# Hybrid decoder trunk on one core: the odd layer in two token ranges, with less MLP filler per round

## The chip, the cores and the metric

The kernel runs on one core of a Trainium2 chip. The metric is the device time of one execution in microseconds (us); lower is better. The time before is 2784.98 us, the median of three executions from 2773.43 to 2786.07 us. The traced execution took 2783.84 us.

The engines are named as in the profile: PE (TensorE, the matmuls) with PEld (its weight loads), DVE (VectorE), ACT (ScalarE), POOL (GpSimd), and SP, whose queue issues the DMAs. `Lnnn` is a line of the kernel.

## The reference

Two layers over 1024 tokens of width 1024, each a mixer and then a squared-ReLU MLP (width 4096), each behind an RMSNorm. The even layer's mixer (sparse attention and pooling) is not touched. What matters is the odd layer, a gated DeltaNet, cut to its core:

```python
p = h @ w_in                                    # q, k, v, z: 8 heads of 128 each; b, a: one per head
qkv = silu(causal_depthwise_conv(qkv, conv_w))  # 4 taps along the tokens
q = l2norm(q) * 128 ** -0.5;  k = l2norm(k)
beta = sigmoid(b);  g = cumsum(-exp(a_log) * softplus(a + dt_bias))   # per head
tmat = inverse(I + strict_lower(beta * (k k^T) * decay))              # per chunk of tokens
value = tmat @ (v * beta);  k_cumdecay = tmat @ (k * beta * exp(g))
# chunk after chunk, with a 128x128 state per head:
v_new = val - kcd @ state;  o = qd @ state + at @ v_new
state = state * gl + kd^T @ v_new
y = (rmsnorm(o, o_norm) * silu(z)) @ w_out
h = h + y
h = h + square(relu(rmsnorm(h, mlp_norm) @ w1)) @ w2
```

The kernel takes chunks of 128 tokens, so each range of 512 tokens has four.

## The kernel before, in words

Tokens lie in two ranges of 512, `s = 0` and `s = 1`; the residual `h[s]` is eight 128x512 tiles. All wide products are made of three matmuls at 128x512 (`mm3`, lines L245, L246, L247): high part by high part, high by low, low by high. Each 128x512 tile of weights is loaded by a DMA into `raw`, copied to its high part by ACT (L165), and its low part is subtracted by POOL (L169). The projections of the odd layer and its output use weight tiles named `w`, the MLP uses `wm`.

`odd_heads` runs 16 head jobs, eight for each range. A head job (`odd_head`) is a generator of 17 steps, a chain that goes back and forth between PE, DVE and ACT: transposes (L977, L989, L995), the decay matrix (L1004 is one matmul per head and serves below as the head's mark), the products of keys and queries (L1018, L1020), the inversion by levels (L1044 and L1050 four times, L1070 and L1074 twice), four chunks through the state (L1088 to L1097) and the output transposes (L1116). Up to three head jobs are in flight, started at least eight rounds apart. In a round every active head makes a step, an output product (`output`, rows `ps_d<-y,w` and `ps_d<-yh,w`) may make two, a projection for a later head (`project`, rows `ps_g<-x,w`) may make one, and a share of MLP work, the filler, is written in between so that PE has something to do while a head's chain is on another engine.

The filler is `mlp_half`, the MLP of one layer on one range: per piece either 24 matmuls of the first product (rows `ps_g<-xb,wm` or `ps_g<-x,wm`, priced `T_COLS` = 5.6) or 6 of the second (rows `ps_d<-y,wm`, priced `T_ROWS` = 1.4). There are two: "below" is the even layer's MLP on range 1, which must end before the odd layer can read `h[1]`; "above" is the odd layer's MLP on range 0, which needs all of `h[0]`'s odd-layer output. `FILL = (5.6, 4.7)` is what a round gets while "below" and while "above" is in use.

The 16 head jobs form one list: the projection of range 1's head 0 may start while range 0's heads 6 and 7 are under way. Before it, all that is left of "below" is written out, then the norm of `h[1]` (`norm_stages`: squares, their sums by matmuls at L288, a reciprocal root in small DVE steps at L264 to L269, its spread over the partitions by transposes at L276, then eight scaled and split tiles). "above" starts when range 0's four output products are done; its own norm goes first. What is left of "above" after the last head goes beside the last norm of `h[1]`, and then the odd layer's MLP on range 1 runs alone.

The text in which the program is written is not the final order: a scheduler moves instructions, so that single filler matmuls stand between the small ones of a head. The order is told below.

Of the kernel before, what the change touches and what calls it, by code (L numbers as in the profile page):

```python
# [25 lines left out]
NH = 8  # L26
# [5 lines left out]
TOPK = 256  # L32
LEVELS = (2, 4, 8, 16, 32, 64)
STAGGER = 8
FILL = (5.6, 4.7)
EARLY = 7
BANKS = {"even": {"g": 2, "o": 1, "s": 1, "t": 4}, "odd": {"g": 2, "o": 1, "d": 2, "t": 3}}

# [11 lines left out]
R_MIX = 0  # L50
R_MLP = 16
# [73 lines left out]
class Trunk:  # L125
# [123 lines left out]
    def project(self, key, x, cols=P, tag="g", st="a"):  # L249

        ps = self.bank(tag)
        for n, w in enumerate(self.columns(key, st, cols)):
            for j in range(KT // 2):
                k = n * KT // 2 + j
                self.mm3(ps[:cols], w[0][:, j], w[1][:, j], x[k][:, 0:512], x[k][:, 512:1024], k == 0, k == KT - 1)
        self.tick(self.pace)
        return ps
# [865 lines left out]
    def odd_heads(self, fills):  # L1123


        seq = [(s, h) for s in range(2) for h in range(NH)]
        x, G, qkvz, ys = [[], []], [None, None], {}, {}
        outs, written = deque(), [0, 0]

        def project(i):  # L1130
            s, h = seq[i]
            if h == 0 and s == 1:
                yield from self.norm_stages(self.h[s], R_MIX + 8, x[s])
                yield
            t = []
            for n in range(4):
                while self.live == self.Q.n:
                    yield
                t.append(self.odd_project(s, h, n, x[s]))
                yield  # L1140
                if h == 0 and n == 1:
                    G[s] = self.odd_gates(x[s], self.grow)
                    yield
            qkvz[i] = t

        def output(s, h):
            for _ in range(5):
                yield
            a = [ys.pop((s, h - 1 + n)) for n in range(2)]
            yield from self.accumulate(("oo", s, h // 2), "o", a, s)  # L1150
            written[s] += 1

        def head(i):
            s, h = seq[i]
            yield from self.odd_head(s, h, *qkvz.pop(i), G[s], ys)
            if h % 2:
                outs.append(output(s, h))

        def step(gen):
            return next(gen, self) is not self  # L1160

        self.live = 0
        norm = self.norm_stages(self.h[0], R_MIX + 8, x[0])
        ahead, nxt, fill, due, above = None, 2, fills[0](), 0.0, False
        for n in (4, 2, 2):
            next(norm, None)
            for _ in range(n):
                next(fill)
        for _ in chain(project(0), project(1)):
            next(fill)  # L1170
        active, started, done, age = [], 0, 0, 0
        while done < len(seq) or outs:
            if started in qkvz and (not active or (len(active) < 3 and age >= STAGGER)):
                active.append(head(started))
                started, age = started + 1, 0
            age += 1
            for g in list(active):
                if not step(g):
                    active.remove(g)
                    done += 1  # L1180
            for _ in range(2):
                if outs and not step(outs[0]):
                    outs.popleft()
            if not above and fill is None and written[0] == NH // 2:
                fill, due, above = fills[1](), 0.0, True
            if fill:
                due += FILL[above]
                while fill and due > 0:
                    t = next(fill, None)
                    if t is None:  # L1190
                        fill = None
                    else:
                        due -= t
            if ahead is None and nxt < len(seq) and nxt < done + 3:
                if seq[nxt] == (1, 0) and fill:
                    for _ in fill:
                        pass
                    fill = None
                ahead, nxt = project(nxt), nxt + 1
            if ahead and not step(ahead):  # L1200
                ahead = None
        self.room("m", self.WM)
        while any(t[3] is not self.WM for t in self.ready["m"]):
            next(fill)
        return fill
# [188 lines left out]
    def run(self):  # L1394
        a, b = self.odd_units()
        m = [self.mlp_units(l) for l in range(2)]
        early, rest = self.mlp_units(0, 0, EARLY, 4), self.mlp_units(0, 2 * EARLY)
        self.plan(a=self.even_units() + a, o=b, m=early + rest + m[0] + m[1] + m[1])
        self.after_early = len(rest) + 3 * len(m[0])
        self.h = [[None] * KT, [None] * KT]  # L1400
        with ExitStack() as st:
            self.banks("even", st)
            self.even()
        self.banks("odd", self.stack)
        XB = Ring(self.pool("second"), "xb", 8, 1024)
        x = []
        norm = self.norm_stages(self.h[1], R_MLP, x, XB)

        def rest():
            fill = self.mlp_half(0, 0, self.x0, [self.Y], 2 * EARLY)  # L1410
            for n in (0, 2, 3):
                for _ in range(n):
                    yield next(fill)
                next(norm, None)
            yield from fill

        self.alone(rest(), "below", 3 * len(m[0]))
        below = lambda: self.mlp_half(0, 1, x, [self.Y])

        def above():  # L1420
            xa = []
            for _ in self.norm_stages(self.h[0], R_MLP + 8, xa, XB):
                yield FILL[1]
            yield from self.mlp_half(1, 0, xa, [self.Y])

        fill, x = self.odd([below, above]), []
        for _ in self.norm_stages(self.h[1], R_MLP + 8, x):
            for _ in range(4):
                next(fill, None)
        for _ in fill:  # L1430
            pass
        self.finish(0)
        self.alone(self.mlp_half(1, 1, x, [self.Y]), "above", 0)
        self.finish(1)
# [59 lines left out]
```

## Time and profile before

| | |
|---|---|
| median of three executions | 2784.98 us |
| the profiled execution | 2783.84 us |
| its span, first to last instruction | 2782.1 us |
| mean granted PE clock over the span | 0.978 of full |
| PE busy | 2653.8 us, 95% of the span |
| DVE, ACT, POOL busy | 60%, 43%, 44% |
| odd layer's head jobs, first to last head mark (L1004) | 1016.6 to 2203.0 us |
| MLP of range 1 alone at the end | from about 2425 us |

The span is 1.7 us below the execution's own time. PE's busy time joins overlapping records: matmuls follow each other faster than one record lasts, so a "busy" PE is not one at its peak. The granted clock is a mean over the stretch; 1.00 means it was never lowered there.

### The profile page before, as it was taken

To read this page: it belongs to the slowest core of one execution; us is meant where nothing else is said; L and a number is where in the kernel's file an instruction comes from. 1 tells how busy PE (TensorE), PEld (TensorE's weight loads), DVE (VectorE), ACT (ScalarE), POOL (GpSimd) and SP (SyncE) were. 2 spreads that over 40 slices of the span, in tenths; PEclk is the share of its full clock that TensorE was granted. 3 is DMA by queue.
4 is the path that set the end of the run, shared out by engine and by line. 5 is a ranking of instruction groups with operands and counts; after the bars stand their busy time and mean duration, and the time that the engine had idled before them with its cause. 6 is when DMAs were issued, how large, how long until landed. Compare 5 with 4: busy or idle time off the path is not lost. (4 is left out here: it accounts for less than half of the span.)

```text
span 2782.1 us, 44603 instructions
## 1 busy us (share of the span) xinstructions
PE 2653.8 (95%) x16640; PEld 2094.9 (75%) x16640; DVE 1660.1 (60%) x3587; ACT 1185.8 (43%) x2480; POOL 1227.5 (44%) x1062
## 2 busy tenths in 40 slices
PE   8789989999999999999999999999999999899998
PEld 6566768787777787777777767777777777688886
DVE  5788998734435655655565777655556645633334
ACT  4557767334444543433333344433334333433332
POOL 4653354542245444434454444434444434544442
PEclk9999989999999999999999999999999999999999
DMA  5221223331123222222222212122222222333332
GB/s 192 76 75 35 68 81 98 91 91 54 42 76 96 80 84 73 80 77 78 68 88 73 62 47 64 59 65 77 75 71 73 69 69 87 118 98 95 96 98 76
DMA packets 121068, 220.91 MB, mean 79 GB/s; under 512 B 14098, under 2 KB 15250, under 8 KB 120850
## 3 DMA queue, kind: packets, MB, share of 16 engines
q1 hardware_dynamic: 120850, 218.05, 25.4%
q8 instruction: 131, 2.15, 0.3%
q14 instruction: 87, 0.71, 0.1%
HBM read 209.61 MB, written 4.19 MB: 77 GB/s over the span
## 5 line engine op out<-in xcount | busy, mean ns | idle before, releaser
L169 POOL TENSOR_TENSOR wm<-raw,wm 128x512 fp32r<-128x512 f32 x425 | 562.0, 1323 | 853.9 <-ACT wm L165 840.3
L165 ACT ACTIVATE wm<-raw 128x512 fp32r<-128x512 f32 x425 | 267.3, 629 | 606.2 <-PE ps_g L246 270.7
L169 POOL TENSOR_TENSOR w<-raw,w 128x512 fp32r<-128x512 f32 x222 | 296.7, 1337 | 351.3 <-ACT w L165 330.8
L841 DVE TENSOR_TENSOR h<-ps_d,h 128x512 f32<-128x512 f32 x392 | 267.1, 685 | 134.4 <-PE ps_d L247 132.4
L245 PE MATMUL ps_g<-x,w 128*128 128x512 f32 x644 | 259.5, 403 | 12.1 <-ACT w L165 9.1
L827 DVE SCALAR_TENSOR_TENSOR ps_g<-ps_g,temps 128x512 f32<-128x512 f32 x128 | 89.1, 696 | 291.0 <-ACT temps L825 291.0
L246 PE MATMUL ps_g<-x,w 128*128 128x512 f32 x644 | 257.1, 399 | 4.3 <-DVE x L380 4.1
L247 PE MATMUL ps_g<-x,w 128*128 128x512 f32 x644 | 256.6, 398 | 1.0 <-POOL w L169 1.0
L245 PE MATMUL ps_d<-y,wm 128*128 128x512 f32 x596 | 243.7, 409 | 10.3 <-DVE h L841 8.7
L165 ACT ACTIVATE w<-raw 128x512 fp32r<-128x512 f32 x222 | 139.0, 627 | 258.3 <-PE ps_g L246 180.9
L247 PE MATMUL ps_d<-y,wm 128*128 128x512 f32 x596 | 236.5, 397 | 0.3 <-POOL wm L169 0.2
L246 PE MATMUL ps_d<-y,wm 128*128 128x512 f32 x596 | 236.0, 396 | 0.0
L245 PE MATMUL ps_g<-xb,wm 128*128 128x512 f32 x512 | 207.7, 406 | 5.6 <-ACT qkvz L947 5.0
L247 PE MATMUL ps_g<-xb,wm 128*128 128x512 f32 x512 | 206.4, 403 | 5.5 <-POOL wm L169 5.4
L246 PE MATMUL ps_g<-xb,wm 128*128 128x512 f32 x512 | 205.7, 402 | 0.0
L949 DVE SCALAR_TENSOR_TENSOR qkvz<-temps,conv,qkvz 128x512 f32<-128x512 f32 x144 | 130.8, 909 | 97.9 <-ACT qkvz L947 96.8
L245 PEld LDWEIGHTS ps_g<-x,w 128*128 128x128 f32 x644 | 123.2, 191 | 40.6 <-ACT w L165 9.9
L245 PE MATMUL ps_g<-x,wm 128*128 128x512 f32 x352 | 141.5, 402 | 7.7 <-ACT wm L165 2.9
L246 PEld LDWEIGHTS ps_g<-x,w 128*128 128x128 f32 x644 | 123.0, 191 | 33.3 <-DVE x L380 6.6
L245 PEld LDWEIGHTS ps_d<-y,wm 128*128 128x128 f32 x596 | 112.0, 188 | 44.9 <-DVE h L841 16.9
L246 PE MATMUL ps_g<-x,wm 128*128 128x512 f32 x352 | 140.9, 400 | 4.4 <-DVE x L169 4.4
L247 PE MATMUL ps_g<-x,wm 128*128 128x512 f32 x352 | 141.1, 401 | 3.2 <-POOL wm L169 3.2
(445 smaller groups left out, 6089.5 us busy)
## 6 DMA issues: line engine op xcount, KB each, us to landing
raw<-in_w_dram SPq DMA_DIRECT2D x456, 256.0 KB, 2.7
raw<-in_woi_dram SPq DMA_DIRECT2D x128, 256.0 KB, 2.6
raw<-in_w2q_dram SPq DMA_DIRECT2D x56, 256.0 KB, 2.6
raw<-in_wei_dram SPq DMA_DIRECT2D x52, 256.0 KB, 2.7
raw<-in_weo_dram SPq DMA_DIRECT2D x32, 256.0 KB, 2.7
raw<-in_woo_dram SPq DMA_DIRECT2D x32, 256.0 KB, 2.7
h<-in_xt_dram SPq DMA_DIRECT2D x16, 256.0 KB, 3.0
at<-at SPq DMA_DIRECT2D x64, 64.0 KB, 2.0
```

The lines of the kernel that those rows point to most:

```text
L165: self.nc.scalar.activation(out, in_, AF.Copy)
L169: eng.tensor_tensor(lo, full, hi.bitcast(F32), op=OP.subtract)
L245: mm(ps, wh, xh, start=start, stop=False)
L246: mm(ps, wh, xl, start=False, stop=False)
L247: mm(ps, wl, xh, start=False, stop=stop)
L827: nc.vector.scalar_tensor_tensor(ps, ps, 0.0, r, op0=OP.max, op1=OP.mult)
L841: nc.vector.tensor_tensor(h, ps, h, op=OP.add)
L949: nc.vector.scalar_tensor_tensor(acc, pin[:, j:j + 512], cw(j), acc, op0=OP.mult, op1=OP.add)
```

## The change

`odd_heads` becomes a loop over the two ranges. In each range: the norm of `h[s]` with 4, 2 and 2 filler pieces in its three stages, the projections of head 0 with a filler piece at each step, and then rounds until all eight heads and their outputs are done. There are no heads of both ranges in flight together any more. A round's filler is 3.5 when no projection is under way at that point and 2.8 when one is. After range 0, the norm for "above" stands with four pieces of "below" in each of its stages, all the rest of "below" is written out, and "above" becomes the filler from then on, so that it lies beside the norm of `h[1]` and the first projections of range 1. The normed input of range 1 goes into the ring `XB` that "below" read from, and "above" reads from `self.X`; before it was the other way round. The last norm also writes into `XB`.

No arithmetic is added or left out: there are as many matmuls as before.

```diff
-FILL = (5.6, 4.7)
+FILL = (3.5, 2.8)
...
-        seq = [(s, h) for s in range(2) for h in range(NH)]
-        x, G, qkvz, ys = [[], []], [None, None], {}, {}
-        outs, written = deque(), [0, 0]
-        def project(i):
-            s, h = seq[i]
-            if h == 0 and s == 1:
-                yield from self.norm_stages(self.h[s], R_MIX + 8, x[s])
-                yield
...
+        def filled(us):
+            self.due += us
+            while self.due > 0:
+                self.due -= next(fill, 1e9)
...
-        for _ in chain(project(0), project(1)):
-            next(fill)
-        active, started, done, age = [], 0, 0, 0
-        while done < len(seq) or outs:
...
-            if not above and fill is None and written[0] == NH // 2:
-                fill, due, above = fills[1](), 0.0, True
-            if fill:
-                due += FILL[above]
...
-            if ahead is None and nxt < len(seq) and nxt < done + 3:
-                if seq[nxt] == (1, 0) and fill:
-                    for _ in fill:
-                        pass
-                    fill = None
-                ahead, nxt = project(nxt), nxt + 1
+        for s in range(2):
+            self.due, G = 0.0, {}
+            norm = self.norm_stages(self.h[s], R_MIX + 8, xs[s], (self.X, self.XB)[s])
+            for n in (4, 2, 2):
+                next(norm, None)
+                for _ in range(n):
+                    next(fill)
+            for _ in project(s, 0, G):
+                next(fill)
+            active, started, done, age, ahead, nxt = [], 0, 0, 0, None, 1
+            while done < NH or outs:
...
+                filled(FILL[ahead is not None])
+                if ahead is None and nxt < NH and nxt < done + 3:
+                    ahead, nxt = project(s, nxt, G), nxt + 1
...
+            if s == 0:
+                xa = []
+                norm = self.norm_stages(self.h[0], R_MLP + 8, xa)
+                for _ in range(3):
+                    next(norm, None)
+                    for _ in range(4):
+                        next(fill, None)
+                for _ in fill:
+                    pass
+                fill = fills[1](xa)
...
-        def above():
-            xa = []
-            for _ in self.norm_stages(self.h[0], R_MLP + 8, xa, XB):
-                yield FILL[1]
-            yield from self.mlp_half(1, 0, xa, [self.Y])
+        above = lambda xa: self.mlp_half(1, 0, xa, [self.Y])
...
-        for _ in self.norm_stages(self.h[1], R_MLP + 8, x):
+        for _ in self.norm_stages(self.h[1], R_MLP + 8, x, XB):
```

How the order moves, at two places. The first is PE at the norm of `h[1]` ahead of range 1's heads, between the sums of squares (L288) and the spread of the root (L276). Before (`y,w` and `yh,w` are the output product of range 0, the others head work):

```order
L288 MATMUL ps_t<-ca,temps 128x2 x4
L246 MATMUL ps_d<-yh,w 128x512
L247 MATMUL ps_d<-yh,w 128x512
L245 MATMUL ps_d<-y,w 128x512
L1070 MATMUL ps_t<-xx_7986,lm 64x64 x4
L246 MATMUL ps_d<-y,w 128x512
L247 MATMUL ps_d<-y,w 128x512
L1074 MATMUL ps_t<-dy,xt 64x64 x4
L1004 MATMUL ps_t<-grow,sel 128x512
L276 MATMUL ps_t<-ca,rs_y 128x128 x4
```

Five wide matmuls and some head work stood between the two. In the changed program, at the same norm (`y,wm` and `x,wm` are the filler "above"):

```order
L288 MATMUL ps_t<-ca,temps 128x2 x4
L245 MATMUL ps_d<-y,wm 128x512
L246 MATMUL ps_d<-y,wm 128x512
L247 MATMUL ps_d<-y,wm 128x512
...
L276 MATMUL ps_t<-ca,rs_y 128x128 x4
L245 MATMUL ps_g<-x,wm 128x512
L246 MATMUL ps_g<-x,wm 128x512
L247 MATMUL ps_g<-x,wm 128x512
```

Eighteen filler matmuls stand there now, and 24 more between L276 and the first projection that reads the normed tiles.

The second place is PE within a range 0 head's window (from the mark L1004 of the range's head 2 to that of head 3), between the end of one level of the inversion (L1050) and the start of the next (L1044), which waits for two DVE steps. Before:

```order
L1050 MATMUL ps_t<-dy,xtc 32x16 x16
L246 MATMUL ps_d<-y,wm 128x512
L247 MATMUL ps_d<-y,wm 128x512
L245 MATMUL ps_d<-y,wm 128x512
...
L1088 MATMUL ps_t<-state,qkvz 128x128
L1093 MATMUL ps_o<-state,qkvz 128x128
L1044 MATMUL ps_t<-xxc,lm 32x16 x16
```

Twenty filler matmuls stood between the two levels. In the changed program:

```order
L1050 MATMUL ps_t<-dy,xtc 32x16
L247 MATMUL ps_d<-y,wm 128x512
L245 MATMUL ps_d<-y,wm 128x512
L246 MATMUL ps_d<-y,wm 128x512
L1088 MATMUL ps_t<-state,qkvz 128x128
L1093 MATMUL ps_o<-state,qkvz 128x128
L1044 MATMUL ps_t<-xxc,lm 32x16 x12
```

Three are left between them; in the same window the filler falls from 190 wide matmuls to 102.

More of the change, by code (lines that the diff above doesn't have):

```diff
@@ L1123, in odd_heads, with step @@
     def odd_heads(self, fills):
-        seq = [(s, h) for s in range(2) for h in range(NH)]
-        x, G, qkvz, ys = [[], []], [None, None], {}, {}
-        outs, written = deque(), [0, 0]
-        def project(i):
-            s, h = seq[i]
-            if h == 0 and s == 1:
-                yield from self.norm_stages(self.h[s], R_MIX + 8, x[s])
-                yield
[L1135 to L1144, printed above, removed]
+        xs, fill = [[], []], fills[0]()
+        qkvz, ys, outs, written = {}, {}, deque(), [0, 0]
+        def step(gen):
+            return next(gen, self) is not self
         def output(s, h):
@@ L1151, in output, with head @@
             written[s] += 1
-        def head(i):
-            s, h = seq[i]
-            yield from self.odd_head(s, h, *qkvz.pop(i), G[s], ys)
+        def head(s, h, G):
+            yield from self.odd_head(s, h, *qkvz.pop(h), G, ys)
             if h % 2:
                 outs.append(output(s, h))
-        def step(gen):
-            return next(gen, self) is not self
-        self.live = 0
-        norm = self.norm_stages(self.h[0], R_MIX + 8, x[0])
-        ahead, nxt, fill, due, above = None, 2, fills[0](), 0.0, False
@@ L1165, in odd_heads @@
-        for n in (4, 2, 2):
-            next(norm, None)
-            for _ in range(n):
-                next(fill)
-        for _ in chain(project(0), project(1)):
-            next(fill)
-        active, started, done, age = [], 0, 0, 0
-        while done < len(seq) or outs:
[L1173 to L1183, printed above, removed]
-            if not above and fill is None and written[0] == NH // 2:
-                fill, due, above = fills[1](), 0.0, True
-            if fill:
-                due += FILL[above]
-                while fill and due > 0:
-                    t = next(fill, None)
-                    if t is None:
-                        fill = None
-                    else:
-                        due -= t
-            if ahead is None and nxt < len(seq) and nxt < done + 3:
-                if seq[nxt] == (1, 0) and fill:
-                    for _ in fill:
-                        pass
-                    fill = None
-                ahead, nxt = project(nxt), nxt + 1
-            if ahead and not step(ahead):
-                ahead = None
@@ new lines, in project @@
+        def project(s, h, G):
+            t = []
+            for n in range(4):
+                while self.live == self.Q.n:
+                    yield
+                t.append(self.odd_project(s, h, n, xs[s]))
+                yield
+                if h == 0 and n == 1:
+                    G.update(self.odd_gates(xs[s], self.grow))
+                    yield
+            qkvz[h] = t
+        def filled(us):
+            self.due += us
+            while self.due > 0:
+                self.due -= next(fill, 1e9)
@@ new lines, in odd_heads @@
+        self.live = 0
+        for s in range(2):
[6 more added lines that the diff above has]
+            for _ in project(s, 0, G):
+                next(fill)
+            active, started, done, age, ahead, nxt = [], 0, 0, 0, None, 1
+            while done < NH or outs:
+                if started in qkvz and (not active or (len(active) < 3 and age >= STAGGER)):
+                    active.append(head(s, started, G))
+                    started, age = started + 1, 0
+                age += 1
+                for g in list(active):
+                    if not step(g):
+                        active.remove(g)
+                        done += 1
+                for _ in range(2):
+                    if outs and not step(outs[0]):
+                        outs.popleft()
+                filled(FILL[ahead is not None])
+                if ahead is None and nxt < NH and nxt < done + 3:
+                    ahead, nxt = project(s, nxt, G), nxt + 1
+                if ahead and not step(ahead):
+                    ahead = None
+            if s == 0:
[8 more added lines that the diff above has]
+                fill = fills[1](xa)
@@ L1404, in run @@
         self.banks("odd", self.stack)
-        XB = Ring(self.pool("second"), "xb", 8, 1024)
+        XB = self.XB = Ring(self.pool("second"), "xb", 8, 1024)
         x = []
```

## Prediction

> **What bounds the kernel now.** The page comes first: it names the engine that carries the time and where it is not full.
>
> ```profile
> span 2782.1 us, 44603 instructions
> PE 2653.8 (95%) x16640; PEld 2094.9 (75%) x16640; DVE 1660.1 (60%) x3587; ACT 1185.8 (43%) x2480; POOL 1227.5 (44%) x1062
> PE   8789989999999999999999999999999999899998
> ```
>
> PE is the bound from the odd layer on (slices 13 to 40), but its digits cannot tell a stretch that loses 2% from one that loses 10%. A better measure is needed. The wide matmuls (128x512, in triples at L245, L246, L247) are the same in number before and after, so I price them at the rate at which a stretch of nothing else runs, and call what is left of a stretch its overhead: the heads' small matmuls, and all waiting. The rate is from the last MLP, alone on PE. The next rows are the windows of the stretch, cut at the heads' marks (each head's L1004), with the instructions of L245 alone: length, busy time and count, weight loads, granted PE clock, DMA. First the price, then the odd layer from its first filler matmul to the end of the program.
>
> ```profile
> 2440.00:2740.00 300.00, 170.79 (x436) 81.87 (x436) 1.00 0.32 95
> ...
> 890.70:1016.60 125.90, 67.17 (x168) 30.89 (x167) 0.99 0.28 86
> 1016.60:1085.40 68.80, 32.82 (x81) 15.21 (x81) 1.00 0.26 77
> 1085.40:1158.50 73.10, 32.22 (x80) 15.03 (x80) 1.00 0.25 77
> 1158.50:1244.60 86.10, 39.69 (x97) 18.65 (x97) 0.98 0.25 74
> 1244.60:1340.20 95.60, 44.59 (x111) 20.77 (x111) 1.00 0.26 78
> 1340.20:1424.70 84.50, 39.07 (x97) 18.22 (x97) 1.00 0.26 76
> 1424.70:1520.20 95.50, 44.54 (x111) 20.77 (x111) 1.00 0.25 78
> 1520.20:1592.20 72.00, 29.69 (x71) 13.77 (x71) 0.98 0.21 63
> 1592.20:1669.00 76.80, 27.58 (x64) 12.12 (x64) 0.93 0.15 46
> 1669.00:1721.40 52.40, 18.67 (x44) 8.72 (x44) 0.97 0.19 56
> 1721.40:1796.00 74.60, 25.95 (x62) 12.28 (x62) 0.91 0.19 61
> 1796.00:1872.90 76.90, 33.65 (x82) 15.81 (x82) 0.98 0.23 69
> 1872.90:1963.50 90.60, 41.10 (x102) 19.16 (x102) 1.00 0.24 76
> 1963.50:2045.00 81.50, 36.04 (x88) 16.82 (x88) 0.98 0.23 72
> 2045.00:2132.60 87.60, 40.38 (x100) 18.78 (x100) 1.00 0.25 76
> 2132.60:2203.00 70.40, 30.86 (x76) 14.28 (x76) 1.00 0.23 69
> 2203.00:2301.20 98.20, 42.91 (x105) 19.78 (x105) 1.00 0.23 68
> 2301.20:2782.10 480.90, 255.78 (x653) 122.55 (x653) 0.99 0.31 96
> ```
>
> 300 us over 436 triples is 0.688 us a triple (0.229 a matmul). A window's overhead is its length less 0.688 times its count: 10.3 for the start (norm of `h[0]`, gates, first projections), 13.1 for the first head's window, where few heads are in flight, then 18.1, 19.4, 19.2, 17.8, 19.1 (mean 18.7) in range 0 with filler. Then come 23.2, 32.8, 22.1 and 31.9 in the four windows from 1520.2 to 1796.0. Range 1 with filler has 20.5, 20.4, 21.0, 18.8, 18.1 (mean 19.8), the last head's tail 26.0, and the rest of the program 31.6. Together 383.4 us. So the place that loses is the passage from range 0 to range 1: its four windows are 110.0 where four windows at 19.2 would be 76.8, about 33 us over.
>
> What stands in that passage is read from PE's waits, first in it (220 us), then in the 690 us before it; columns are total, times, longest.
>
> ```profile
> PE ps_t L276 <- DVE rs_y L269: 4.0, 2, 2.6
> PE ps_t L1044 <- DVE xxc L1037: 2.6, 1, 2.6
> PE ps_t L1090 <- DVE vb L1089: 2.4, 3, 1.7
> PE ps_o L1094 <- ACT vn L165: 2.1, 2, 1.8
> ...
> PE ps_d L245 <- DVE h L841: 4.3, 7, 1.7
> PE ps_g L245 <- ACT qkvz L947: 3.0, 3, 1.0
> PE ps_t L276 <- DVE rs_y L269: 2.6, 1, 2.6
> ```
>
> In the passage PE waits for the heads' own chains (`xxc`, `vb`, `vn`) and for the norm's root (`rs_y`); with filler the chains are no longer among the waits. By the order there is no filler matmul at all from the end of the 1520.2 window to the middle of the 1721.4 one. The other part of the 33 us is the clock: 0.93, 0.97 and 0.91 of full in these three windows are at most 0.07 x 76.8 + 0.03 x 52.4 + 0.09 x 74.6 = 13.7 us of lost PE time.
>
> **The change, part by part.** All sums are against the profiled execution's 2783.84 us, 1.1 below the median.
>
> The wide matmuls keep their number, so they cost the same wherever they stand, as long as dense filler runs at its price. The part of "below" that is left after range 0 is about 60 us (264 matmuls by the order), written out with the usual four `wm` tiles. A weight tile of 12 matmuls (2.75 us on PE) needs one DMA of SP's queue, an ACT copy and a POOL subtraction, which move with it:
>
> ```profile
> L169 POOL TENSOR_TENSOR wm<-raw,wm 128x512 fp32r<-128x512 f32 x425 | 562.0, 1323 | 853.9 <-ACT wm L165 840.3
> L165 ACT ACTIVATE wm<-raw 128x512 fp32r<-128x512 f32 x425 | 267.3, 629 | 606.2 <-PE ps_g L246 270.7
> 2301.00:2353.00 52.00, 50.98 (x224) 41.43 (x223) 25.64 (x38) 20.78 (x35) 23.21 (x18) 1.00 0.28 88
> 2353.00:2390.00 37.00, 34.06 (x151) 26.58 (x150) 22.03 (x41) 14.00 (x25) 20.39 (x16) 1.00 0.26 81
> ```
>
> 1.32 us of POOL hides under 2.75, and the stretch after the last head, filler and output with the same tiles, is 52.0 us for 224 matmuls at 0.229 = 51.3. Dense filler is therefore taken at its price. The window behind it holds the last norm under filler: 37.0 less 139 wide matmuls at 0.229 (31.8) is 5.2. I take 6.0 for the norm of "above", which gets the same cover.
>
> Now each range is like the one before with cover: a start, a first window, six windows, a tail. Range 0: 10.3 + 13.1 + 6 x 18.7 + 26.0 = 161.6. Norm of "above": 6.0. Range 1: a start at 10.3 (its norm has eighteen filler matmuls between sums and spread, 4.1 us, as range 0's start has, and that still waited the 2.6 us shown), 13.1, 6 x 19.8, 26.0 = 168.2. The rest 31.6. Sum 367.4, which is 16.0 below 383.4: the 33 us come back, less the 17 that a second drain and a second start cost. The ring swap costs nothing: the scaled tiles of range 1 go into `XB`, whose last reader, the first product of "below", ends 72 filler matmuls or more (16 us) before. If that cover were gone, the eight tiles would be late by a norm, bounded by the 10.3 of a start.
>
> Against this stands the thinner filler. By the order a head's window has 106 filler matmuls on average in either range, where range 0 had 192 and range 1 162. What that costs is not in the trace; it is bounded by the window with no filler, 1669.0 to 1721.4, whose overhead is 22.1, and by the filled ones. On a straight line range 0's windows would gain (22.1 - 18.7)/192 x 86 = 1.5 us each and range 1's (22.1 - 19.8)/162 x 56 = 0.8; with seven windows each (the tail counted as one) that is 16 us, all of the gain. If a chain needs only a few filler matmuls to be covered, it is nothing: in the order most waits of a head keep two to four wide matmuls in between, and what goes is taken out of runs of twenty. Within the filled windows neither reading wins (18.1 with 80 triples, 19.2 with 111). I take the middle, 8 us. DVE does not become the bound:
>
> ```profile
> 1158.50:1244.60 86.10, 85.68 (x666) 68.34 (x665) 50.00 (x114) 32.49 (x78) 37.55 (x38) 0.98 0.25 74
> 1669.00:1721.40 52.40, 48.66 (x505) 37.77 (x504) 37.56 (x95) 23.36 (x63) 21.21 (x24) 0.97 0.19 56
> ```
>
> It is busy 50.0 of 86.1 us with filler and 37.6 of 52.4 without; halfway, some 44 of 66. A change of PE between wide and small matmuls costs it too, but there are some 34 such changes in a head's window of either order.
>
> So: 2783.84 - 16.0 + 8 = 2776 us.
>
> One rule is weighed here. The granted clock fell to 0.91 in a window whose longest PE wait was 2.6 us. The Trainium skill (TensorE: Matmul & The Clock Gate, HAM oscillation) has the clock drop after idle gaps above about 3.4 us; by that alone the 13.7 us would not be tied to the waits and would not come back, and the sum would be 2790. Its next section (A second HAM failure mode) says that frequent short idling between groups does it as well; the trace agrees with that one, and by it the sum stays. The same section speaks against this change, since thinner filler means more short idling in every head: rival four.
>
> **The rivals.**
> 1. The thin filler costs nothing. For it: the order, and the 18.1 of the window with 80 triples. Against it: range 1, with less filler than range 0, has the higher mean. Time: 2784 - 16 = 2768.
> 2. Slower: the heads' chains come to light in every window, as in the passage. Three filler matmuls (0.7 us) where there were twenty may be less than two DVE steps need behind other heads' DVE work; PE waits there, in order, and all filler and projections behind it wait too. Price: every window at the unfilled 22.1, that is 6 x 3.4 + 6 x 2.3 = 34 us, against 16 gained: 2802. It decides from 1.2 us a window on (14 windows with the tails); at 2.1 it is slower by more than 0.5%. Against it: the window without any filler reaches 22.1 only with a clock of 0.97.
> 3. The passage is not cured, because norms and gates, not missing filler, make it: the two windows with a norm are at 32.8 and 31.9, the one without at 22.1. Then the excess of these two over 19.8, 25.1 in all, stays in place of the 10.3 and 6.0 set for them, and the time is 2776 + 9 = 2785. Against it: start and last norm under filler cost 10.3 and 5.2.
> 4. Every head's window gets one stretch of lowered clock: the windows at 0.98 lost some 0.02 x 86.1 = 1.7 us. Ten more of them are 17 us on the flat sum of 2768: 2785.
>
> **How the numbers follow.** Chances: forecast 0.36, rival 1 0.30, rival 2 0.12, rival 3 0.13, rival 4 0.09. Half a per cent, 14 us, is about what a measurement of this kernel tells from no change. Faster than 2771: most of rival 1 and the lower edge of the forecast, 0.32. Slower than 2799: most of rival 2, 0.12 with what I have not seen. The rest 0.56. The range is from 2764, rival 1 with the norm of "above" wholly hidden and a little over, to 2800, just under rival 2; the forecast's own range is 2768 to 2784.
>
> **What would show it.** Right: no window between the first and the last mark without filler, no granted clock under 0.97 around the passage, a sum of overheads near 375; the head windows of both ranges at 19 to 21; the waits of L1044, L1090 and L1094 on `xxc`, `vb` and `vn` small; after range 0 a stretch of `ps_g<-xb,wm` and `ps_d<-y,wm` at 0.229 us a matmul. Wrong: head windows at 22 and above, or waits of `ps_g` and `ps_d` on `wm` in the dense stretch, or a start of range 1 well above 10.3 us, with L276 waiting on `rs_y` and the projections on `xb`.

## The result, and the profile after

The changed kernel takes 2763.34 us, median of six executions (2759.34 to 2765.03), against 2778.85 for six of the kernel before: a ratio of 0.9938, 95% interval 0.9923 to 0.9954. It is 0.6% or 15.5 us faster. The forecast was 2776 with a range from 2764; the measured time lies 0.7 us below that range; the nearest rival is the first, at 2768.

The page of the changed kernel, as far as it answers to the lines shown of before:

```profile
span 2762.7 us, 44636 instructions
PE 2637.2 (95%) x16640; PEld 2084.1 (75%) x16640; DVE 1665.5 (60%) x3587; ACT 1187.5 (43%) x2480; POOL 1228.9 (44%) x1062
PE   8789989999999999999999999999999999999998
```

As the prediction said of such digits, they cannot tell the two kernels apart. First comes a stretch that the change does not touch: all that lies ahead of the odd layer's first filler matmul. The two rows are that stretch in the kernel before and in the changed one (length, then PE, PEld, DVE, ACT, POOL, clock, DMA).

```profile
0.00:890.70 890.70, 825.37 (x3984) 644.13 (x3985) 597.62 (x1330) 477.97 (x917) 397.20 (x305) 0.96 0.27 83
...
0.00:886.40 886.40, 820.08 (x3984) 641.17 (x3985) 597.76 (x1330) 477.78 (x917) 397.59 (x305) 0.97 0.27 83
```

The same instructions took 4.3 us less in the execution that was profiled after. This is spread, not the change: over the profiled executions of all fourteen kernels here, which share this stretch, it takes 881.5 to 892.1 us. Of the 19.4 us between the two spans only 15.1 lie in the changed part. The same windows as in the prediction, cut at the heads' marks, L245 alone (length, busy, count, weight loads, clock, DMA):

```profile
886.40:987.00 100.60, 50.99 (x128) 23.11 (x128) 1.00 0.27 82
987.00:1055.10 68.10, 32.53 (x81) 15.22 (x81) 1.00 0.26 78
1055.10:1113.40 58.30, 21.23 (x51) 9.84 (x51) 0.97 0.19 60
1113.40:1180.40 67.00, 27.41 (x68) 12.77 (x68) 1.00 0.22 68
1180.40:1261.40 81.00, 36.29 (x90) 16.92 (x90) 1.00 0.24 76
1261.40:1326.60 65.20, 26.33 (x64) 12.24 (x64) 0.97 0.22 66
1326.60:1405.00 78.40, 33.65 (x82) 15.69 (x82) 0.98 0.22 68
1405.00:1458.90 53.90, 21.12 (x51) 9.59 (x51) 1.00 0.24 70
1458.90:1744.00 285.10, 141.59 (x353) 66.03 (x353) 0.99 0.26 79
1744.00:1812.30 68.30, 32.58 (x81) 15.23 (x81) 1.00 0.26 78
1812.30:1865.50 53.20, 20.70 (x51) 9.60 (x51) 1.00 0.20 65
1865.50:1930.00 64.50, 27.43 (x68) 12.77 (x68) 1.00 0.23 70
1930.00:2009.60 79.60, 36.44 (x90) 16.91 (x90) 1.00 0.26 77
2009.60:2072.90 63.30, 26.10 (x64) 12.03 (x64) 1.00 0.23 68
2072.90:2149.40 76.50, 33.19 (x82) 15.40 (x82) 1.00 0.23 70
2149.40:2203.70 54.30, 21.06 (x51) 9.59 (x51) 1.00 0.23 64
2203.70:2289.30 85.60, 36.22 (x90) 16.86 (x90) 1.00 0.20 59
2289.30:2762.70 473.40, 254.00 (x648) 122.04 (x648) 0.98 0.32 97
```

At 0.688 us a triple the overheads are: start 12.5, first window 12.4, range 0's six windows 23.2, 20.2, 19.1, 21.2, 22.0, 18.8 (mean 20.8), the passage 42.2, first window 12.6, range 1's six 18.1, 17.7, 17.7, 19.3, 20.1, 19.2 (mean 18.7), tail 23.7, rest 27.6. The sum is 367.6, against 383.4 before. The sum that the prediction had before it added anything for thin filler was 367.4.

PE's waits (total, times, longest), first in the passage (1459 to 1744), then in range 0's windows (1055 to 1459), then the largest in range 1's (1812 to 2204):

```profile
PE ps_t L276 <- DVE rs_y L269: 3.7, 1, 3.7
PE ps_d L245 <- DVE h L841: 3.3, 4, 1.3
PE ps_t L1090 <- DVE vb L1089: 1.5, 1, 1.5
...
PE ps_g L247 <- POOL wm L169: 4.1, 4, 3.1
...
PE ps_t L1090 <- DVE vb L1089: 2.0, 1, 2.0
...
PE ps_t L1050 <- DVE dy L1047: 2.3, 3, 1.2
```

The chains' waits of the passage are nearly gone, the root's wait is not. Range 0 has a wait of another kind: for the low parts of filler weights, 3.1 us in one piece.

### The profile page after: what moved, and what is told of

Its sections match the earlier page's. It is cut to its first block, busy times and chain, and to the rows that moved or that the text cites. A ratio compares the mean times of both kernels' runs of the same rounds, so it can differ in the third digit from the quotient of the medians.

```text
span 2762.7 us, 44636 instructions
## 1 busy us (share of the span) xinstructions
PE 2637.2 (95%) x16640; PEld 2084.1 (75%) x16640; DVE 1665.5 (60%) x3587; ACT 1187.5 (43%) x2480; POOL 1228.9 (44%) x1062
## 4 chain that ended last, share of the span: by engine, by line
PE 53%; DVE 6%; ACT 1%; issue 1%; POOL 0%; DMA 0%; DVEq 0%; POOLq 0%; ACTq 0%
PE ps_g L245 9%; PE ps_g L246 9%; PE ps_g L247 9%; PE ps_d L245 6%; PE ps_d L247 5%; PE ps_d L246 5%; PE ps_t L246 1%; PE ps_t L245 1%; PE ps_t L247 1%; DVE h L841 1%; PE ps_t L1050 1%; PE ps_t L1044 1%; DVE qkvz L949 1%; PE ps_o L1094 1%; PE ps_t L1074 1%
## 5 line engine op out<-in xcount | busy, mean ns | idle before, releaser
L245 PE MATMUL ps_d<-y,wm 128*128 128x512 f32 x596 | 246.1, 413 | 14.5 <-DVE h L841 12.9
L247 PE MATMUL ps_d<-y,wm 128*128 128x512 f32 x596 | 241.1, 404 | 1.6 <-POOL wm L169 1.2
L246 PE MATMUL ps_d<-y,wm 128*128 128x512 f32 x596 | 239.3, 402 | 0.0
L245 PE MATMUL ps_g<-x,wm 128*128 128x512 f32 x476 | 191.7, 403 | 8.2 <-ACT wm L165 2.9
L246 PE MATMUL ps_g<-x,wm 128*128 128x512 f32 x476 | 190.6, 400 | 4.4 <-DVE x L169 4.4
L247 PE MATMUL ps_g<-x,wm 128*128 128x512 f32 x476 | 190.2, 400 | 3.8 <-POOL wm L169 3.7
L245 PE MATMUL ps_g<-x,w 128*128 128x512 f32 (+1 forms) x388 | 155.9, 402 | 12.2 <-ACT w L165 8.8
L246 PE MATMUL ps_g<-x,w 128*128 128x512 f32 (+1 forms) x388 | 154.3, 398 | 5.2 <-DVE x L380 4.1
L247 PE MATMUL ps_g<-xb,wm 128*128 128x512 f32 x388 | 153.0, 394 | 4.4 <-POOL wm L169 4.2
L245 PE MATMUL ps_g<-xb,wm 128*128 128x512 f32 x388 | 153.0, 394 | 0.4 <-ACT qkvz L953 0.4
L247 PE MATMUL ps_g<-x,w 128*128 128x512 f32 (+1 forms) x388 | 153.2, 395 | 0.0
L246 PE MATMUL ps_g<-xb,wm 128*128 128x512 f32 x388 | 152.9, 394 | 0.0
L245 PEld LDWEIGHTS ps_d<-y,wm 128*128 128x128 f32 x596 | 112.7, 189 | 44.7 <-DVE h L841 15.3
L247 PEld LDWEIGHTS ps_d<-y,wm 128*128 128x128 f32 x596 | 113.0, 190 | 27.0 <-POOL wm L169 3.6
L841 DVE TENSOR_TENSOR h<-ps_t,h 128x512 f32<-128x512 f32 x128 | 88.1, 689 | 69.4 <-PE ps_t L247 69.0
```

The lines of the kernel that those rows point to most:

```text
L245: mm(ps, wh, xh, start=start, stop=False)
L246: mm(ps, wh, xl, start=False, stop=False)
L247: mm(ps, wl, xh, start=False, stop=stop)
L841: nc.vector.tensor_tensor(h, ps, h, op=OP.add)
```

## The experiments

Theory A: the gain is cover for the passage, and thin filler costs a head's window nothing. Theory B: thin filler has a price, as the prediction had it. Times are medians; ratios are to the kernel before, run beside each group (its medians were 2776 to 2778).

### The structure alone

```diff
-FILL = (3.5, 2.8)
+FILL = (5.6, 4.7)
```

> Two ranges as in the changed kernel, but with the old amounts of filler in a round, FILL = (5.6, 4.7). By the order a head's window has 156 to 192 filler matmuls in place of 96 to 126, and the passage between the ranges still has 288 in place of 798. Theory A (the gain is the cover of the passage; thin filler costs nothing): 2763 us, within 5 us of the changed kernel, a ratio of 0.994 to the kernel before. Theory B (thin filler costs about 8 us, as the prediction had it): 8 us faster than the changed kernel, 2755 us, 0.991.

Measured: 2861.71 us, ratio 1.0297 (1.0281 to 1.0313). Both theories missed it by some 100 us. The windows of the second to sixth head of range 0 as one row, then the passage, the second tail and the rest, and PE's longest wait in the tail:

```profile
1070.60:1502.90 432.30, 192.87 (x475) 90.06 (x475) 0.99 0.24 74
...
1576.70:1784.70 208.00, 76.45 (x182) 34.89 (x182) 0.87 0.18 55
...
2377.20:2453.90 76.70, 16.90 (x40) 7.65 (x40) 0.78 0.15 42
2453.90:2864.70 410.80, 208.56 (x526) 100.17 (x526) 0.94 0.29 89
...
PE ps_t L1116 <- DVE delta L1112: 7.0, 2, 4.5
```

The five windows have 105.5 us of overhead, 21.1 each, as much as with thin filler. But the filler is used up when it is needed most: the tail has 40 triples in place of 90 and 49.2 us of overhead in place of 23.7, the passage 82.8 in place of 42.2, the rest 48.9 in place of 27.6, with the clock at 0.78 to 0.94. That is 87 of the 98 us. My expectation had counted 288 filler matmuls in the passage and did not see that most of them are range 1's start, and none left beside range 0's last heads. The prediction never priced this either: without the smaller amounts the two ranges lose 3%.

### The amounts alone

```diff
 # the kernel before
-FILL = (5.6, 4.7)
+FILL = (3.5, 2.8)
```

> The kernel before with FILL = (3.5, 2.8) and nothing else: one list of 16 heads, no filler in the windows around the passage, 111 to 126 filler matmuls in a filled head's window in place of 190. Theory A: as the kernel before, 2779 us within 5 us, ratio 1.000; the passage keeps its 33 us of excess. Theory B: 8 us or more slower, 2787 us, 1.003.

Measured: 2781.37 us, ratio 1.0006 (0.9994 to 1.0019): no change. Range 0's five full windows, the four windows of the passage, and PE's largest wait in the former:

```profile
1064.10:1434.10 370.00, 154.58 (x373) 72.44 (x373) 0.97 0.22 68
1434.10:1794.00 359.90, 154.19 (x379) 71.33 (x379) 0.98 0.22 69
...
PE ps_d L247 <- POOL w L169: 6.0, 2, 3.0
```

The overhead is 113.4, or 22.7 a window against 18.7 with thick filler: range 0 does pay, 20 us. The four windows of the passage have 99.1 in place of 110.0, with what was left of "below" written out beside the last heads, and smaller gains lie behind it, so that the whole hardly moves. Theory A's number is met, but by two effects that cancel. So neither theory is whole: a price is there, but PE's largest waits in these windows are for weights (9.1 us with those for `wm`), not for a head's chain.

### No filler in the rounds

```diff
-FILL = (3.5, 2.8)
+FILL = (0.0, 0.0)
```

> Two ranges with FILL = (0, 0): no filler in any round; all of it is written out after each range's heads, still beside the norms. It prices a head's window with no filler. Theory A: the chains come to light in all 14 windows and two tails; at the 22.1 of the one unfilled window of the kernel before, 16 x 3 = 48 us more than the changed kernel, 2811 us; at twice that excess, 2860. If the filler in the rounds is worth nothing at all: 2763.

Measured: 2878.19 us, ratio 1.0356 (1.0340 to 1.0372), beyond the dearest case. The rows are five windows of range 0, then five of range 1, its last window, and the tail:

```profile
1022.20:1251.60 229.40, 73.44 (x176) 33.90 (x176) 0.99 0.17 52
...
1832.00:2057.50 225.50, 74.26 (x177) 33.81 (x177) 0.98 0.17 53
2057.50:2104.90 47.40, 8.52 (x19) 3.86 (x19) 0.70 0.12 35
2104.90:2168.50 63.60, 7.26 (x13) 3.29 (x13) 0.63 0.06 17
```

The windows with projections are 21.7 and 20.7 us, hardly more than with any filler. The last window, after the projections, is 34.3 and the tail 54.7, at a clock of 0.70 and 0.63. The loss sits where a range's projections are over.

### No cover in the passage

```diff
-                for _ in range(n):
+                for _ in range(n if s == 0 else 0):
                     next(fill)
             for _ in project(s, 0, G):
-                next(fill)
+                if s == 0:
+                    next(fill)
...
-                norm = self.norm_stages(self.h[0], R_MLP + 8, xa)
-                for _ in range(3):
-                    next(norm, None)
-                    for _ in range(4):
-                        next(fill, None)
                 for _ in fill:
                     pass
+                for _ in self.norm_stages(self.h[0], R_MLP + 8, xa):
+                    pass
```

> The changed kernel, but the passage has no cover: all of filler below is written out before the norm of filler above, that norm stands alone, and the norm of range 1 and the first projections have no filler beside them. Rounds are filled as in the changed kernel. Theory A: the two norms and the first projections come to light; each norm is a chain of some 8 us from sums to the first scaled tile plus the squares, so 15 to 25 us more than the changed kernel, 2778 to 2788 us, about the kernel before. Theory C (norms cost what they cost, covered or not): 2763 us.

Measured: 2796.87 us, ratio 1.0067 (1.0053 to 1.0081): 33.5 us more than the changed kernel. Its passage, and the two longest waits there:

```profile
1458.10:1725.20 267.10, 119.91 (x297) 55.86 (x297) 0.94 0.23 71
...
PE ps_t L288 <- DVE temps L308: 14.4, 1, 14.4
PE ps_t L276 <- DVE rs_y L269: 5.0, 2, 2.5
```

The overhead of the passage is 62.8 in place of 42.2, 20.6 us. The norms and first projections cost this when bare, in one wait of 14.4 us at the sums of squares above all. Theory C falls. The rest, 13 us by the medians and 17 between the two profiled executions, lies in range 1's windows, the tail and the end, where the filler falls in other places.

### Filler on one side only

```diff
-FILL = (3.5, 2.8)
+FILL = (3.5, 0.0)    # e6: only without a projection
+FILL = (0.0, 2.8)    # e9: only beside a projection
```

> The changed kernel with FILL = (3.5, 0): filler only in rounds in which no projection is under way. A head's window falls to 37 to 94 filler matmuls from 96 to 126; the heads after the last projection keep theirs. Theory A (any wide matmul covers the chains, so filler matters only where projections are over): 2763 us within 5. Theory B (a head's window needs its filler): at the 3 us a window that no filler cost in the head windows of the kernel before, 12 windows give up to 36 us, 2780 to 2799.

> The counterpart, FILL = (0, 2.8): filler only in rounds with a projection, none once a range's last projection is written. Theory A: the head windows stay at 19 to 22, and the two tails lose their cover: with no filler at all they and what lies behind them cost 30 us each more (54.3 against 24.6; 79.3 against 43.7), with the last windows 11 to 15 us each, so 60 to 85 us more than the changed kernel, 2823 to 2848 us. Theory B: no place is special, and the loss is spread over the windows.

Measured: e6 2809.59 us, ratio 1.0119 (1.0103 to 1.0136); e9 2831.64, 1.0198 (1.0180 to 1.0216). Five windows of range 0, its last window and the passage, of e6 and then of e9:

```profile
1039.00:1340.30 301.30, 116.83 (x285) 54.43 (x285) 0.99 0.21 64
1340.30:1387.70 47.40, 14.04 (x33) 6.46 (x33) 0.92 0.18 57
1387.70:1754.40 366.70, 184.93 (x459) 86.68 (x459) 0.98 0.27 80
...
1048.50:1321.10 272.60, 101.27 (x248) 46.79 (x248) 0.99 0.20 61
1321.10:1369.80 48.70, 13.50 (x31) 6.29 (x31) 0.89 0.16 44
1369.80:1768.70 398.90, 193.61 (x483) 91.23 (x483) 0.96 0.25 78
```

e9 came out as theory A had it: windows at 20.4, the last one at 27.4, the passage at 66.6. e6 did not: its windows stay at 21.0, but the last window is 24.7, since it has 54 filler matmuls for 102, the passage 50.9, and the first windows and the end lose too; it is 46 us slower, where theory A had no change and theory B 36 us at most. Part of this is a wait of another kind: between 886 and 2400 us PE waits 8.8 us there for low parts of `w` from POOL, up to 3.0 in one piece, as in e2. The windows of the second to sixth head put side by side (range 0, range 1; in the old order's range 1 the third to seventh; filler matmuls in a window by the order):

| kernel | filler in a window | overhead, range 0 | range 1 |
|---|---|---|---|
| before | 144 to 194 | 18.7 | 19.8 |
| changed | 96 to 126 | 21.1 | 18.6 |
| e1, two ranges, thick | 156 to 192 | 21.1 | 21.5 |
| e2, old order, thin | 84 to 126 | 22.7 | 19.4 |
| e6 | 37 to 94 | 21.0 | 20.3 |
| e9 | 24 to 54 | 20.4 | 19.0 |
| e3 | 0 | 21.7 | 20.7 |

There is no line in it from thick to none. In these windows, which have projections, the means differ by 4.0 us at most, and not by the amount of filler. The dear windows are a range's last ones, behind the projections, where filler is short: 24.7 in e6, 27.4 in e9, 34.3 in e3. The chains are not wholly covered either: PE's waits for the heads' own chains sum to 10.9 and 10.3 us in e3's two sets of five windows, about 2 us a window.

### The products that stand in POOL's queue

In the changed kernel's range 0, ACT, POOL and then PE, from the timeline (start, length, engine, instruction, idle time before and what ended it):

```profile
1059.46 0.63 ACT L165 ACTIVATE wm<-raw 128x512 fp32r<-128x512 f32 x1 [0.54 <-issue]
...
1060.64 1.28 POOL L1025 TENSOR_TENSOR qkvz<-qkvz,delta 128x512 f32<-128x512 f32 x1 [11.22 <-PE ps_t L1020]
1061.88 1.26 POOL L1026 TENSOR_TENSOR qkvz<-qkvz,delta 128x512 f32<-128x512 f32 x1
1063.11 1.31 POOL L169 TENSOR_TENSOR wm<-raw,wm 128x512 fp32r<-128x512 f32 x1
...
1064.47 0.50 PE L247 MATMUL ps_g<-xb,wm 128*128 128x512 f32 x1 [3.07 <-POOL wm L169]
```

POOL sat for 11.2 us at a head's product that waited for PE. ACT had the weight's high part ready at 1060.09, but its low part stood behind both products and started at 1063.11, 3.0 us later; PE waited 3.07 us for it.

```diff
-        nc.gpsimd.tensor_tensor(k, k, e, op=OP.mult)
-        nc.gpsimd.tensor_tensor(q, q, e, op=OP.mult)
+        ve.tensor_tensor(k, k, e, op=OP.mult)
+        ve.tensor_tensor(q, q, e, op=OP.mult)
```

> The changed kernel with the two products by the decay (k by e and q by e in odd_head) on DVE in place of POOL. In the changed kernel's range 0 PE waits 4.1 us for low parts of filler weights, at worst 3.1 us in one piece: the subtraction stood on POOL behind these two products (2.5 us), which had waited 11 us for PE's L1020. If that queue is what makes range 0's windows 21.1 against 19.0 in range 1, they fall to about 19.5 and the kernel to 2753 to 2758 us. If the windows differ for another reason, or DVE's 1.4 us more per head cost as much: 2763 us within 4.

> The kernel before with the two products by the decay on DVE, nothing else. Theory P (products on POOL cost PE time only where filler is thin, because weights behind them in POOL's queue are then needed sooner): 2778 us within 4, ratio 0.999 to 1.001, since PE's waits for POOL are 4.6 us in the whole odd layer there. Theory Q (they cost in every kernel): as much as the 19 us they gave in the changed kernel, 2759 us.

> The old order with FILL = (3.5, 2.8), as in e2, and the two products on DVE. Its range 0 windows with a full set of heads had overheads of 26.1, 18.0, 26.6, 19.8 and 24.6 us, 23.0 on average, against 18.7 in the kernel before. Theory P: these fall to about 19, so some 15 us under e2's 2781, 2766 us. If thin filler costs by the heads' own chains, range 0 stays at 23 and the kernel at 2781.

Measured: in the changed kernel (e5) 2744.08 us, ratio 0.9882 (0.9866 to 0.9899), 19 us under the changed kernel, twice the largest gain expected, and the fastest of all; in the kernel before (e10) 2772.99, 0.9991 (0.9979 to 1.0004), nothing; in the old order with thin filler (e11) 2760.44, 0.9947 (0.9932 to 0.9962), 21 us under e2. Five windows of range 0 and of range 1 in e5, then of range 0 in e11:

```profile
1060.00:1398.20 338.20, 143.59 (x355) 66.72 (x355) 1.00 0.23 70
...
1802.70:2139.10 336.40, 143.70 (x355) 66.71 (x355) 1.00 0.23 71
...
1061.90:1415.80 353.90, 151.33 (x373) 70.50 (x373) 1.00 0.23 71
```

The overheads are 18.8 and 18.4 in e5 (21.1 and 18.6 before the edit), and 19.5 in e11 (22.7 in e2). By the two traces PE's order, from the odd layer's first filler matmul on, differs between the changed kernel and e5 in 153 of 12,656 rows. So theory P's forecast holds: the products on POOL cost next to nothing beside thick filler and about 20 us beside thin. PE's waits for low parts from POOL (900 to 2300 us) go the same way: 9.7 us in e2 and 0.6 in e11, 5.6 in the changed kernel and 2.0 in e5, 4.6 in the kernel before and 3.7 in e10. What range 0 pays for thin filler goes with the products on POOL, and the collision in POOL's queue is the cause that the waits show.

How much of the gain is this collision is less sure. In the profiled executions e5 is 20 us faster from the first filler matmul on: 11.7 in range 0's five windows, 3.5 behind the last mark, the rest in pieces of about 1 us. Only 3.6 us are shown waits for POOL; those for `h` fell by 6.6 and for `vb` by 3.0, and the three windows at a clock of 0.97 and 0.98 are at 1.00. That a product is also shorter on DVE (0.68 us, against 1.28 in the row above) was not separated from the queue; against it speaks range 1, where filler is as thin and the windows hardly gained. Why the collision falls into range 0 is open.

### More filler at the root

```diff
-            for n in (4, 2, 2):
+            for n in (4, 5, 2):    # e7; e8 with the products on DVE
+            for n in (4, 5, 6):    # e12, with the products on DVE
```

> The changed kernel with 4, 5 and 2 in place of 4, 2 and 2 pieces of filler in the stages of the norm ahead of each range's heads: 48 wide matmuls in place of 18 between the sums of squares (L288) and the spread of the root (L276). The changed kernel's PE waits 2.6 us there in range 0 and 3.7 us in range 1. If those waits are lost time, 6 us come back, and up to 3 more if the clock stays up: 2754 to 2758 us. If DVE only takes the filler's additions into the same queue and the root comes later by as much: 2763 us.

> The changed kernel with the two products on DVE and with 4, 5 and 2 pieces in the norm's stages. The pieces alone made the changed kernel 9 us slower (2772 us), though PE no longer waits at the root. If that loss is the collision of weights with POOL's products, as other places in the rounds then meet, it goes with the products: 2738 to 2744 us. If the pieces cost by themselves: 2752 us.

> The changed kernel with the two products on DVE and 4, 5 and 6 pieces in the norm's stages: 48 wide matmuls ahead of the spread of the root as in e8, and 54 between it and the first projection, where e8 had 12 and e5 24. In e5 PE waits 2.6 and 3.6 us for the root; in e8 it waits 11 us for scaled tiles and the first projections instead. If the norm needs cover on both sides and nothing else differs, both waits go: 2736 to 2742 us, under e5's 2744. If what e7 and e8 lost lies in the rounds and the end of the program, which the pieces shift: 2755 to 2760 us again.

Measured: e7 2772.07 us, ratio 0.9975 (0.9961 to 0.9989), 9 slower than the changed kernel; e8 2759.07, 0.9938 (0.9923 to 0.9954), and e12 2768.82, 0.9969 (0.9959 to 0.9979), 15 and 25 slower than e5. All three lie above every time that was expected for them, and e8 shows that what the pieces cost is not the collision with the products. In e8 PE no longer waits for the root. At range 1's start it waits for these instead:

```profile
PE ps_g L246 <- POOL xb L169: 2.3, 3, 1.7
PE ps_g L245 <- ACT qkvz L947: 1.8, 2, 1.6
```

The order shows why: the wide matmuls behind the root, ahead of the first projection, fell from 24 to 12, so PE met the unfinished tiles. e12 has cover on both sides; its starts lose those waits, but its windows and first windows came out dearer. So the missing cover behind the root is not the whole of the loss. Of e8's, 8.0 us lie behind the last mark (an overhead of 56.4 against 48.4 in e5). Why these pieces shift so much elsewhere was not settled.

## Why the prediction was wrong

**The measure and the place: right.** Pricing wide matmuls at 0.229 us and adding up the overheads gave 367.4 before any penalty; 367.6 was measured. That the two agree to 0.2 us is luck, since parts of the sum are off by up to 12 us and make up for each other. The 33 us of the passage came back less the second tail and start: the passage was set at 26.0 + 6.0 + 10.3 = 42.3 and is 42.2. e4 shows that the cover does it.

**The thin filler: the term that was mis-sized.** This is the step that failed first. I put 8 us between a flat reading and a straight line from the unfilled window; the sum of overheads shows 0.2. Thin filler was not free for that: range 0's six windows rose by 12 us on the 18.7 that the sum had set, and as much came back where I had forecast none, 7 in range 1's windows (on 19.8), 6 in the tail and the rest. Range 0's rise is not the price of thin filler by itself: e5 takes all of it away with the filler as thin as before (its six windows have 112.2 us, as the sum had set them). What lowered the other parts is shown only in pieces: two of range 1's windows had a clock of 0.98 before and 1.00 now, and behind the last mark PE's waits for POOL's `wm` (2.1 us) and at L1116 (1.9) are gone. The straight line was drawn through a window of the passage (22.1), whose lack of filler was not its only trait: it came right after a norm. Rival 2's mechanism is small in a window with projections: waits for the chains are about 2 us a window with no filler (e3) and under 1 with thin filler (3.7 and 3.6 us in e5's two sets of five). Rival 4's clock loss was confined to three windows of range 0, at 0.97 to 0.98.

**The base.** This is the other failed step. The sum was made against the profiled 2783.84 us. The kernel before has its median at 2776 to 2779 in the larger groups of runs, so that execution was 5 to 8 us late; the 890.7 us that it took up to the odd layer are near the end of their spread. With the flat sum and that base the forecast would have been 2760 to 2763. The 8 us for thin filler and 5 us of base (2783.84 against 2778.85) make up the 12.7 us that the forecast missed by.

**Cover for the norms: half right.** The wait at range 1's root was set as 2.6 us, like range 0's, and is 3.7; the same eighteen matmuls stand there. More cover there did not pay: not with less left behind the root (e7, e8), and not with cover on both sides (e12).

**What was not asked.** Of each part I priced what it costs, not what it would be alone. e1 and e2 show that one loses 3%, the other gives nothing, and both together gain. With the products on DVE the second gains alone: e11 takes 2760.44 us where e10 takes 2772.99.

**The weighed rule.** The clock came back to 0.99 over the passage, and where cover was taken away it fell to 0.63 to 0.87 (e1, e3). This speaks for the reading that the lowered clock follows the waits. In e3 the longest wait of the tail is 4.5 us, so those rows cannot separate the two sections of the Trainium skill (TensorE: Matmul & The Clock Gate); the changed kernel's window from 1261.4 to 1326.6, at 0.97 with a longest wait of 1.3 us, can, and it sides with A second HAM failure mode.

## What to carry to other kernels

Filler is worth most where a chain has nothing else beside it: after the last projection, at a norm, in a drain. Count what is left for those places before choosing how much to spend per round; in rounds that had wide work of their own, the means here differed by 4 us at most, and not by the amount. When rounds get shorter, look at in-order queues that feed the bound engine: an instruction that waits there for that same engine holds back the operands behind it, and here moving two such products to another engine was worth more (19 us) than the whole change (15.5 us), while in the kernel before it gave nothing.

## What was not expected

Small shifts of where filler pieces fall moved the whole by 9 to 25 us (e7, e8, e12) with the same work on every engine, more than most terms of the sum. A single profile of one such order therefore says little about another; the overhead per window, compared over seven orders, said more.
